# Seven block products for eight in the up-projection of a two-layer decoder trunk: four K blocks of every second strip pair, spread among the plain tiles of two strips

## The chip, the cores and the metric

The kernel runs on one core of one Trainium2 chip. The metric is the device time of one execution in microseconds. The core's engines work side by side, each through a queue of its own: TensorE (PE) multiplies matrices, VectorE (DVE) and ScalarE (ACT) work on elements, GpSimd (POOL) and SyncE (SP) issue transfers here. An instruction that needs another engine's result waits for it at the head of its queue.

## The reference

Two layers over 256 tokens of width 2048. Layer 0 has stick-breaking attention, layer 1 dilated window attention over shared keys and values; each is followed by a gated feed-forward part with a causal convolution and a gate on a per-layer embedding. The change touches the feed-forward part alone, and of it only the product with `w_up`:

```
D_FF = 5632
def causal_depthwise_conv(u, w, bias):        # width 3, along the tokens
    ...
def conv_ffn(h, w_up, conv_w, conv_b, w_down):
    u = causal_depthwise_conv(h @ w_up, conv_w, conv_b)
    gate, val = u[..., :D_FF], u[..., D_FF:]
    return (jax.nn.silu(gate) * val) @ w_down
```

`h` is the normed stream, 256 x 2048; `w_up` is 2048 x 11264. All inputs are 32-bit floats.

## The kernel before, in words

**The work of a matmul.** K, the summed dimension of 2048, is cut into 16 blocks of 128; the tokens into two blocks of 128; the columns of a weight into strips of 512. For 32-bit accuracy every operand is split in a high and a low part, and a block product is three matmuls into one bank of PSUM: low x high, high x low, high x high (`add_block`, lines 339 to 341 before, 342 to 344 after). The tokens' parts are made once; they are the tiles `h`, one for each K block. The weights' parts are made tile by tile.

**A strip.** `weights` (from line 274, line 285 for the transfer) loads a raw buffer of four K blocks of a strip, 1 MB, through SyncE's queue into one of four buffers (`raw`). Two K blocks at a time make a tile: ScalarE copies it into a high part (`whi`, line 302), VectorE subtracts that to get the low part (`wlo`, line 303). There are four buffers for each. So a strip has 8 tiles of 12 matmuls (two K blocks, two token blocks, three matmuls), 96 in all. `strip_v` runs a strip, with its two sums (`accv`, one bank for each token block) in a pool of five banks; one more tile, `two`, holds two banks, and one bank is left for other uses.

**A strip pair.** Strip s gives gate columns, strip s + 11 (`s + FB // 4`) value columns. `products` yields the strips in turn, gate and value alternating. When a strip's sums are complete, ScalarE scales them out of PSUM (`scaled`, line 406), VectorE transposes them in blocks (line 240), and GpSimd sends them to memory and back (lines 243 and 251), which turns the tokens into the free dimension. `finish_strip` convolves a strip one strip later (lines 771 to 780). For a value strip it also multiplies with the gate (line 793) and splits the result into four blocks for the down-projection.

**Parts.** A layer's 11 strip pairs come in two parts, 5 pairs and then 6, each followed by the down-projection of its part. In a layer's first part the first pair starts on the 12 K blocks that are ready (`late` in `products`).

**Order.** The program is written in one stream; a scheduler puts it into the engines' queues by priority. Splits of weights have a high priority (`tc.high_priority`), so that they stand ahead of the convolutions of the strip before. Waits are set by tile: whoever uses a tile waits for the instructions that wrote or read it before.

Of the kernel before, what the change touches and what calls it, by code (L numbers as in the profile page):

```python
# [47 lines left out]
MAGIC = 1.5 * 2.0 ** 23  # L48


def _two_pi_parts():
# [12 lines left out]

RAW = 4
WARM = 9
NRING, NRAW, NWSP = 40, 4, 4
AHEAD = 200
PI_PARTS = _two_pi_parts()

# [2 lines left out]
def tile_trunk(ctx, tc, head_d, xT_d, x_d, pT_d, pos_d, vec_d, cst_d, csb_d, wqkv, wo_a, wkv, wq_b, wo_b, wup, wdn, wpg, wpp, gfin_d, out_d):  # L73
# [11 lines left out]
    def nm(s):  # L85
        uid[0] += 1
        return f"{s}_{uid[0]}"
# [143 lines left out]
    def four(s):  # L231

        return tt(s, (P, 4 * S), tag="four", bufs=3)
# [99 lines left out]
            add_block(ps[o], xs[k], min(o, 1), hi[:, c], lo[:, c], k == 0 and not begun, ends and k == n - 1)  # L333
        return ps

    def add_block(ps, x, t, hi, lo, first, final):
        xh = x[:, t * P : (t + 1) * P]
        xl = x[:, S + t * P : S + (t + 1) * P]
        nc.tensor.matmul(ps, xl, hi, start=first, stop=False)  # L339
        nc.tensor.matmul(ps, xh, lo, start=False, stop=False)  # L340
        nc.tensor.matmul(ps, xh, hi, start=False, stop=final)  # L341

    def two_strips(W, strips, xs, before, block):

# [11 lines left out]
    def products(jobs, xs, late=None, at=0, then={}, side=2):  # L356

        jobs = list(jobs)
        if late is not None:
            n = len(xs)

            def add():
                with tc.issue_after(last["high"]), tc.issue_after(last["low weights"]):
                    late()

            def before(k0):
                if k0 == at:
# [16 lines left out]
            ready = None  # L389
            if at is None:  # L390
                W, s, base = jobs[0]
                ready = list(weights(W, s, 4, base=base + n))
                add()
            for b, (W, s, base) in zip(begun, jobs):
                yield strip_v(W, s, xs[n:], base + n, begun=b, ready=ready)
                ready = None
            jobs = jobs[side:]
        for W, s, base in jobs:
            yield strip_v(W, s, xs, base)

    def scaled(ps, rc, room):

# [357 lines left out]
    def ffn(i, xs, late, rc):  # L760
        cv = V_CONV + i * 4 * 2 * FB

        def taps(r, j, n=1):
            c = cv + r * 2 * FB + j
            return vec[:, c : c + n]

        def conv_turned(j, z, y):

            runs = y.rearrange("p o (a r) -> p o a r", r=32)
            for o in range(4):  # L770
                nc.scalar.activation(runs[:, o], z[:, :, o], AF.Identity, scale=taps(2, j + o), bias=taps(3, j + o))
                for d in (1, 2):
                    c = runs[:, o, :, d:]
                    nc.vector.scalar_tensor_tensor(c, z[:, :, o, : 32 - d], taps(2 - d, j + o), c, op0=OP.mult, op1=OP.add)  # L774
            for d in (1, 2):
                over = tt("over", (P, 7, 4, 2), bufs=2)[:, :, :, :d]
                w = taps(2 - d, j, 4).unsqueeze(1).unsqueeze(3).to_broadcast([P, 7, 4, d])
                nc.vector.tensor_tensor(over, z[:, :7, :, 32 - d :], w, op=OP.mult)
                c = y.rearrange("p o (a r) -> p a o r", r=32)[:, 1:, :, :d]
                nc.vector.tensor_tensor(c, c, over, op=OP.add)  # L780

        def part(strips, late=None):

            gs = []
            gate = [None]

            def finish_strip(value, s, z):
                y = four("val" if value else "gate").rearrange("p (o c) -> p o c", o=4)
                conv_turned(4 * s + value * FB, z, y)
                if not value:  # L790
                    gate[0] = y
                    return nc.scalar.activation(y, y, AF.Silu).ins
                nc.vector.tensor_tensor(y, y, gate[0], op=OP.mult)
# [23 lines left out]
        half = FB // 4 // 2  # L817
        gs, late, _ = part(range(half), late)
# [221 lines left out]
```

## Time and profile before

| | |
|---|---|
| time, median of 3 runs | 2302.58 us (2302.34 to 2302.81) |
| span of the profiled execution, first to last instruction | 2298.6 us; the median lies 4.0 us above it |
| up-projection, layer 0 | 377.5 to 595.1 us and 703.9 to 965.1 us |
| up-projection, layer 1 | 1471.3 to 1689.5 us and 1798.3 to 2059.5 us |
| busy in 703.9 to 965.1 us (261.2 us) | PE 261.2, DVE 179.05, ACT 145.9, POOL 38.27 us |

The profiled execution has no other time than its span. In the profile's rows stand the start, the duration, the engine, the line, the operation and the tiles (out<-in). "Busy" merges overlapping instructions of an engine; a matmul's row includes its latency, so that rows of neighbouring matmuls overlap. In the waits, "A <- B: total, times, longest" means that A stood idle until B was done. In stretch tables there is one column of busy time for each engine, and (xN) counts instructions.

### The profile page before, as it was taken

How to read it: one execution, taken by the hardware profiler on the slowest of the kernel's cores; microseconds unless marked ns; L12 is line 12 of the kernel's file. 1: busy time of each engine (PE TensorE's matmuls, PEld its weight loads, DVE VectorE, ACT ScalarE, POOL GpSimd, SP SyncE). 2: the span in 40 equal slices, each digit the busy share in tenths (PEclk: the TensorE clock that was granted, in tenths of full speed). 3: DMA queues.
4: the chain of work that ended last, by engine and by line, in shares of the span. 5: the costliest groups of instructions: out<-in, count | busy, mean ns of one | idle time of the engine just before them, and what ended most of it. 6: DMA issues, size and time to landing. Idle time of an engine off the chain costs nothing.

```text
span 2298.6 us, 27859 instructions
## 1 busy us (share of the span) xinstructions
PE 2286.6 (99%) x10197; PEld 1893.6 (82%) x10197; DVE 1514.4 (66%) x2205; ACT 1257.3 (55%) x1680; POOL 328.4 (14%) x575
## 2 busy tenths in 40 slices
PE   9999999999999999999999999999999999999998
PEld 7888888888888888888888888888888888888887
DVE  7666666676754767765677665767675476776565
ACT  6554555655534555644565554565553465554554
POOL 0311111111100111101111331211110011110100
PEclk9999999999999999999999999999999999999999
DMA  8777667767656677767577776777765577776763
GB/s 308 254 236 250 221 240 249 247 239 246 223 199 208 241 245 240 244 205 246 205 263 240 252 262 216 262 253 242 237 237 188 215 237 243 244 238 211 239 226 119
DMA packets 98346, 538.44 MB, mean 234 GB/s; under 512 B 16672, under 2 KB 17568, under 8 KB 46752
## 3 DMA queue, kind: packets, MB, share of 16 engines
q1 hardware_dynamic: 63360, 435.46, 54.2%
q0 software_dynamic: 32560, 95.98, 14.0%
q10 hardware_dynamic: 2288, 5.21, 0.6%
q8 instruction: 80, 1.31, 0.2%
q14 instruction: 58, 0.48, 0.1%
HBM read 486.52 MB, written 50.07 MB: 233 GB/s over the span
## 4 chain that ended last, share of the span: by engine, by line
PE 97%; DMA 1%; ACT 1%; DVE 0%; issue 0%; POOL 0%; SPq 0%; ACTq 0%; DVEq 0%; POOLq 0%
PE accv L340 32%; PE accv L341 31%; PE accv L339 31%; PE two L420 1%; PE two L341 0%; PE two L340 0%; PE two L339 0%; DMA turned<-there 0%; DMA there<-y 0%; PE keys L420 0%; ACT whi L302 0%; DVE wlo L303 0%; DMA vec<-in_head 0%; ACT h L140 0%; POOL turned L251 0%
## 5 line engine op out<-in xcount | busy, mean ns | idle before, releaser
L303 DVE TENSOR_TENSOR wlo<-raw,whi 128x1024 fp32r<-128x1024 f32 (+1 forms) x824 | 1001.7, 1216 | 696.0 <-ACT whi L302 694.9
L302 ACT ACTIVATE whi<-raw 128x1024 fp32r<-128x1024 f32 (+1 forms) x824 | 867.8, 1054 | 910.4 <-PE accv L341 886.7
L341 PE MATMUL accv<-whi,h 128*128 128x512 f32 x2328 | 905.3, 389 | 0.0
L339 PE MATMUL accv<-whi,h 128*128 128x512 f32 x2328 | 904.1, 388 | 0.9 <-ACT whi L302 0.6
L340 PE MATMUL accv<-wlo,h 128*128 128x512 f32 x2328 | 904.6, 389 | 0.1
L339 PEld LDWEIGHTS accv<-whi,h 128*128 128x128 f32 x2328 | 437.0, 188 | 92.0 <-ACT whi L302 1.3
L340 PEld LDWEIGHTS accv<-wlo,h 128*128 128x128 f32 x2328 | 437.0, 188 | 91.5 <-DVE wlo L303 1.4
L341 PEld LDWEIGHTS accv<-whi,h 128*128 128x128 f32 x2328 | 437.1, 188 | 89.6
L243 POOL DMA_DIRECT2D there<-y x162 | 91.7, 566 | 1305.5 <-DVE y L240 1288.5
L339 PE MATMUL accv<-whi,g 128*128 128x512 f32 x704 | 273.9, 389 | 0.0
L340 PE MATMUL accv<-wlo,g 128*128 128x512 f32 x704 | 273.9, 389 | 0.0
L341 PE MATMUL accv<-whi,g 128*128 128x512 f32 x704 | 273.9, 389 | 0.0
L251 POOL DMA_DIRECT2D turned<-there x324 | 190.0, 593 | 430.2 <-DMA there<-y 208.0
L339 PEld LDWEIGHTS accv<-whi,g 128*128 128x128 f32 x704 | 132.1, 188 | 27.5
L341 PEld LDWEIGHTS accv<-whi,g 128*128 128x128 f32 x704 | 132.1, 188 | 27.5
L340 PEld LDWEIGHTS accv<-wlo,g 128*128 128x128 f32 x704 | 132.1, 188 | 27.3
L240 DVE STREAM_TRANSPOSE y<-u 128x512 f32<-128x512 f32 x122 | 85.4, 703 | 1.8 <-DMA there<-y 1.4
L339 PE MATMUL accv<-whi,o 128*128 128x512 f32 x200 | 78.0, 390 | 0.0
L341 PE MATMUL accv<-whi,o 128*128 128x512 f32 x200 | 77.9, 390 | 0.0
L340 PE MATMUL accv<-wlo,o 128*128 128x512 f32 x200 | 77.8, 389 | 0.0
L406 ACT ACTIVATE u<-accv,rcol 128x512 f32<-128x512 f32 x102 | 69.2, 678 | 13.7 <-PE accv L341 13.7
L774 DVE SCALAR_TENSOR_TENSOR val<-turned,vec,val 128x248 f32<-128x248 f32 (+1 forms) x176 | 72.2, 462 | 0.0
(163 smaller groups left out, 1179.6 us busy)
## 6 DMA issues: line engine op xcount, KB each, us to landing
raw<-in_wup SPq DMA_DIRECT2D x176, 1024.0 KB, 5.1
raw<-in_wdn SPq DMA_DIRECT2D x88, 1024.0 KB, 4.8
there<-y POOLq DMA_DIRECT2D x171, 256.0 KB, 5.0
turned<-there POOLq DMA_DIRECT2D x324, 128.0 KB, 4.8
raw<-in_wqkv SPq DMA_DIRECT2D x40, 1024.0 KB, 6.6
raw<-in_wpg SPq DMA_DIRECT2D x32, 1024.0 KB, 4.8
raw<-in_wkv SPq DMA_DIRECT2D x24, 1024.0 KB, 5.3
raw<-in_wo_a SPq DMA_DIRECT2D x16, 1024.0 KB, 5.2
```

Of the source, the lines that this page charges most:

```text
L240: last["turned"] = nc.vector.transpose(y.rearrange("p (b o r) -> p o b r", b=4, o=4), strip.rearrange("p (o b c) -> p o b c", o=4, b=4)).ins
L243: nc.gpsimd.dma_start(there[t * P : (t + 1) * P], y)
L251: nc.gpsimd.dma_start(z[32 * b : 32 * b + 32].rearrange("p a o r -> p a (o r)"), back[b])
L302: last["high"] = nc.scalar.activation(hi[:, c], r, AF.Copy).ins
L303: last["low weights"] = nc.vector.tensor_tensor(lo[:, c], r, f32(hi[:, c]), op=OP.subtract).ins
L339: nc.tensor.matmul(ps, xl, hi, start=first, stop=False)
L340: nc.tensor.matmul(ps, xh, lo, start=False, stop=False)
L341: nc.tensor.matmul(ps, xh, hi, start=False, stop=final)
L406: last["out"] = nc.scalar.activation(u, ps[t], AF.Copy, scale=rc[:, t : t + 1]).ins
L420: run.append(nc.tensor.matmul(*args, skip_group_check=True, **kw).ins)
L774: nc.vector.scalar_tensor_tensor(c, z[:, :, o, : 32 - d], taps(2 - d, j + o), c, op0=OP.mult, op1=OP.add)
```

## The change

For every second strip pair the first four of the 16 K blocks are multiplied in another way. The 256 tokens x 512 K values are a 2 x 2 grid of blocks A (two token blocks, two halves of two K blocks). The weights of gate strip s + 1 and value strip v + 1 over these K blocks are a 2 x 2 grid B (two halves of K, two strips). The four blocks of the result C are formed by seven products of sums of blocks instead of eight plain ones:

- `block_sums` makes the four sums of A once for each layer, and splits them (tiles `sum`).
- `Seven.load` fetches the raw buffers of both strips when the value strip v before them begins; they stay in two of the four raw buffers.
- `first` to `fourth` do four products among the plain tiles of strip v, ahead of its tiles 1, 3, 5 and 7 (`HEADS8`). VectorE makes the sums of B in place in the raw buffers (line 439); each factor is split as a tile of weights is, into the same four pairs of buffers (lines 445 and 446). The results lie in `two` (`c11` in its first bank, `c21` in its second) and in two banks named `seven` (`c12`, `c22`). ScalarE copies `c11` and `c12` aside (lines 478 and 485). After the fourth product VectorE combines: line 495 adds `c22` to the first copy, 496 adds that to `c21`, 497 writes `c22` as the second copy minus `c21`, 498 subtracts from `c12`.
- `fifth`, `sixth` and `seventh` add three more products into `c11`, `c21` and `c12`, among the plain tiles of strip s + 1, ahead of its tiles 0, 1 and 3 (`TAILS`).
- Strip s + 1 goes on in `c11` and `c21`, strip v + 1 in `c12` and `c22`, with the 12 K blocks left (6 tiles of 12 matmuls each).

Product by product it is six matmuls (two K blocks, three each). It happens for pairs 3 and 5 of a layer's first part and for pairs 2, 4 and 6 of its second, ten times in all. `HEADS6` is never used. The ring of small buffers grows from 40 to 42, and a tile `part` for the two copies shares the space of `e`. Nothing outside the feed-forward parts moves on any engine, and SyncE and GpSimd issue the same number of transfers.

The core of the diff:

```diff
-    def add_block(ps, x, t, hi, lo, first, final):
+    def add_block(ps, x, t, hi, lo, first, final, again=False):
...
+    class Seven:
...
+        def first(self):
+            gates = two_banks()
+            self.c11, self.c21 = gates[:, 0], gates[:, 1]
+            self.c12, self.c22 = (bank("seven", "acc") for _ in range(2))
+            both = tt("part", (P, 1024), tag="e", bufs=1)
+            self.p, self.q = both[:, :512], both[:, 512:]
+            w = self.parts(self.b11)
+            self.t, self.u = self.b11, self.b12
+            self.add(self.t, self.b11, self.b12)
+            self.add(self.u, self.b12, self.b22)
+            self.product(self.c11, self.token(0, 0), w, True)
+            with tc.high_priority(offset=AHEAD):
+                nc.scalar.activation(self.p, self.c11, AF.Copy)
...
+        def fourth(self):
+            w = self.parts(self.t)
+            self.add(self.t, self.t, self.b21)
+            self.product(self.c22, self.sums[2], w, True)
+            with tc.high_priority(offset=AHEAD):
+                nc.vector.tensor_tensor(self.p, self.c22, self.p, op=OP.add)
+                nc.vector.tensor_tensor(self.c21, self.c21, self.p, op=OP.add)
+                nc.vector.tensor_tensor(self.c22, self.q, self.c21, op=OP.subtract)
+                nc.vector.tensor_tensor(self.c12, self.c12, self.p, op=OP.subtract)
+
+        def fifth(self):
+            self.product(self.c11, self.token(2, 0), self.parts(self.b21))
+
+        def sixth(self):
+            self.product(self.c21, self.token(2, 1), self.parts(self.t))
+
+        def seventh(self):
+            self.product(self.c12, self.sums[3], self.parts(self.b22))
...
-            ups = products([(wup[i], s + v * FB // 4, 0) for s in strips for v in range(2)], xs, late, None)
+            def up_strips():
+                W, now = wup[i], None
+                for j, s in enumerate(strips):
+                    v = s + FB // 4
+                    after = Seven(W, s + 1, v + 1, xs, sums) if j % 2 == (late is not None) and s + 1 in strips else None
...
+                    yield strip_among(W, s, xs, now.go_on() if now else {}, now and [now.c11, now.c21], base)
+                    yield strip_among(W, v, xs, after.begin(tiles) if after else {}, now and [now.c12, now.c22], base)
+                    now = after
+
+            ups = up_strips()
```

**TensorE's queue where a strip ends, before.** The place is layer 0, the end of the second pair's value strip (`accv_3605`) and the start of the next gate strip (`accv_3779`). The rows are the first two matmuls of its last tile and of the next strip's first two tiles; the ten between them have no waits.

```order
L339 MATMUL accv_3605<-whi_3721,h_3297 128x512 [waits Activation_49]
L340 MATMUL accv_3605<-wlo_3722,h_3297 128x512 [waits DVE_49]
...
L339 MATMUL accv_3779<-whi_3775,h_2694 128x512 [waits Activation_49]
L340 MATMUL accv_3779<-wlo_3776,h_2694 128x512 [waits DVE_49]
...
L339 MATMUL accv_3779<-whi_3793,h_2700 128x512 [waits Activation_49]
L340 MATMUL accv_3779<-wlo_3794,h_2700 128x512 [waits DVE_49]
```

Every tile's first matmul waits for ScalarE's high part, its second for VectorE's low part.

**The same place in the change.** `seven_3643` is `c22`, `two_3641` holds `c11` and `c21`. The rows: the last matmul of the fourth product; the start of the value strip's last tile (`accv_3617`); the fifth product; the next strip's first tile; the sixth product; the second tile.

```order
L455 MATMUL seven_3643<-whi_3782,sum_3087 128x512
L342 MATMUL accv_3617<-whi_3797,h_3315 128x512 [waits Activation_49]
L343 MATMUL accv_3617<-wlo_3798,h_3315 128x512 [waits DVE_49]
...
L455 MATMUL two_3641<-whi_3849,h_2700 128x512 [waits DVE_49,Activation_49]
L455 MATMUL two_3641<-wlo_3850,h_2700 128x512
...
L342 MATMUL two_3641<-whi_3861,h_2862 128x512 [waits Activation_49]
L343 MATMUL two_3641<-wlo_3862,h_2862 128x512
...
L455 MATMUL two_3641<-whi_3877,h_2700 128x512 [waits Activation_49]
L455 MATMUL two_3641<-wlo_3878,h_2700 128x512
...
L342 MATMUL two_3641<-whi_3887,h_2868 128x512 [waits Activation_49]
L343 MATMUL two_3641<-wlo_3888,h_2868 128x512 [waits DVE_49]
```

One plain tile stands between the fourth and the fifth product. The fifth product's first matmul waits for both engines, and the low parts `wlo_3850`, `wlo_3862` and `wlo_3878` have no wait of their own; `wlo_3888` is the first that has one again.

**VectorE's queue there, before.** The end of the same value strip and the start of the next gate strip (the names are those of the fence on TensorE before; `y` are the blocks to be turned).

```order
L303 TENSOR_TENSOR wlo_3722<-raw_3703,whi_3721 128x1024 [waits Activation_49]
L303 TENSOR_TENSOR wlo_3776<-raw_3773,whi_3775 128x1024 [waits DMAHW2_49,Activation_49]
L303 TENSOR_TENSOR wlo_3794<-raw_3773,whi_3793 128x1024 [waits Activation_49]
L303 TENSOR_TENSOR wlo_3812<-raw_3809,whi_3811 128x1024 [waits DMAHW3_49,Activation_49]
L240 STREAM_TRANSPOSE y_3742<-u_3737 128x4x4x32 [waits DMASW4_49,Activation_49]
```

Low parts follow each other, each behind its high part.

**VectorE's queue there, in the change.** From the low part of the last plain tile on; `part_3644` holds the two copies, `seven_3642` is `c12`.

```order
L306 TENSOR_TENSOR wlo_3798<-raw_3764,whi_3797 128x1024 [waits Activation_49]
L446 TENSOR_TENSOR wlo_3850<-raw_3619,whi_3849 128x1024 [waits Activation_49]
L306 TENSOR_TENSOR wlo_3862<-raw_3859,whi_3861 128x1024 [waits DMAHW4_49,Activation_49]
L495 TENSOR_TENSOR part_3644<-seven_3643,part_3644 128x512 [waits PE_49]
L446 TENSOR_TENSOR wlo_3878<-raw_3619,whi_3877 128x1024 [waits Activation_49]
L496 TENSOR_TENSOR two_3641<-two_3641,part_3644 128x512 [waits DVE_49]
L498 TENSOR_TENSOR seven_3642<-seven_3642,part_3644 128x512
L497 TENSOR_TENSOR seven_3643<-part_3644,two_3641 128x512 [waits DVE_49]
L306 TENSOR_TENSOR wlo_3888<-raw_3859,whi_3887 128x1024 [waits Activation_49]
```

The four combinations have come in among the low parts, with the sixth product's low part between the first and the second of them; line 498 stands ahead of line 497. The other nine places have the same rows in the same order.

More of the change, by code (lines that the diff above doesn't have):

```diff
@@ L334, in strip_v @@
         return ps
[L336 removed]
+    def add_block(ps, x, t, hi, lo, first, final, again=False):
         xh = x[:, t * P : (t + 1) * P]
         xl = x[:, S + t * P : S + (t + 1) * P]
[L339 to L341 removed]
+        nc.tensor.matmul(ps, xl, hi, start=first, stop=False, skip_group_check=again)
+        nc.tensor.matmul(ps, xh, lo, start=False, stop=False, skip_group_check=again)
+        nc.tensor.matmul(ps, xh, hi, start=False, stop=final, skip_group_check=again)
     def two_strips(W, strips, xs, before, block):
@@ L399, in products, with block_sums @@
             yield strip_v(W, s, xs, base)
+    def block_sums(xs):
+        f = four("whole").rearrange("p (k c) -> p k c", k=4)
+        for k in range(4):
+            nc.vector.tensor_tensor(f[:, k], f32(xs[k][:, :S]), f32(xs[k][:, S:]), op=OP.add)
+        (a11, a21), (a12, a22) = ((f[:, k : k + 2, :P], f[:, k : k + 2, P:]) for k in (0, 2))
+        m = four("sums").rearrange("p (q i c) -> p q i c", q=4, i=2)
+        nc.vector.tensor_tensor(m[:, 0], a21, a22, op=OP.subtract)
+        nc.vector.tensor_tensor(m[:, 1], a11, a21, op=OP.subtract)
+        nc.vector.tensor_tensor(m[:, 2], m[:, 0], a11, op=OP.subtract)
+        nc.vector.tensor_tensor(m[:, 3], m[:, 2], a12, op=OP.add)
+        out = []
+        for q in (0, 2):
+            hi, lo = (rt("sum", dt=F32R) for _ in range(2))
+            src = m[:, q : q + 2].rearrange("p q i c -> p (q i c)")
+            nc.scalar.activation(hi, src, AF.Copy)
+            nc.vector.tensor_tensor(lo, src, f32(hi), op=OP.subtract)
+            for j in range(2):
+                out.append([[t[:, (2 * j + i) * P : (2 * j + i + 1) * P] for t in (hi, lo)] for i in range(2)])
+        return out
@@ new lines, in tile_trunk, with __init__, add, parts @@
+    class Seven:
+        def __init__(self, W, s0, s1, xs, sums):
+            self.strips = W, s0, s1
+            self.sums = sums
+            self.token = lambda k, t: [[xs[k + i][:, c + t * P : c + (t + 1) * P] for c in (0, S)] for i in range(2)]
+        def add(self, out, a, b):
+            with tc.high_priority(offset=AHEAD):
+                nc.vector.tensor_tensor(out, a, b, op=OP.add)
+        def parts(self, r):
+            hi = wsp.tile([P, 2, 512], F32R, tag="hi", name=nm("whi"))
+            lo = wsp.tile([P, 2, 512], F32R, tag="lo", name=nm("wlo"))
+            with tc.high_priority(offset=AHEAD):
+                last["high"] = nc.scalar.activation(hi, r, AF.Copy).ins
+                last["low weights"] = nc.vector.tensor_tensor(lo, r, f32(hi), op=OP.subtract).ins
+            return hi, lo
+        def product(self, ps, left, w, first=False):
+            for i in range(2):
+                xh, xl = left[i]
+                hi, lo = w[0][:, i], w[1][:, i]
+                for j, (x, y) in enumerate(((xl, hi), (xh, lo), (xh, hi))):
+                    begins, ends = first and i == j == 0, first and i == 1 and j == 2
+                    nc.tensor.matmul(ps, x, y, start=begins, stop=ends, skip_group_check=True)
+        def load(self):
+            W, s0, s1 = self.strips
+            raws = []
+            for s in (s0, s1):
+                raw = wraw.tile([P, RAW, 512], F32, tag="raw", name=nm("raw"))
+                nc.sync.dma_start(raw, W[s, 0])
+                raws.append(raw)
+            (self.b11, self.b21), (self.b12, self.b22) = ((r[:, :2], r[:, 2:]) for r in raws)
+        def first(self):
[9 more added lines that the diff above has]
+            self.product(self.c11, self.token(0, 0), w, True)
+            with tc.high_priority(offset=AHEAD):
+                nc.scalar.activation(self.p, self.c11, AF.Copy)
+        def second(self):
+            w = self.parts(self.t)
+            self.add(self.t, self.t, self.b22)
+            self.product(self.c12, self.sums[0], w, True)
+            with tc.high_priority(offset=AHEAD):
+                nc.scalar.activation(self.q, self.c12, AF.Copy)
+        def third(self):
+            self.product(self.c21, self.sums[1], self.parts(self.u), True)
+        def fourth(self):
+            w = self.parts(self.t)
+            self.add(self.t, self.t, self.b21)
+            self.product(self.c22, self.sums[2], w, True)
+            with tc.high_priority(offset=AHEAD):
+                nc.vector.tensor_tensor(self.p, self.c22, self.p, op=OP.add)
[8 more added lines that the diff above has]
+            self.product(self.c12, self.sums[3], self.parts(self.b22))
+        def begin(self, tiles):
+            do = [self.first, self.second, self.third, self.fourth]
+            self.hooks = {0: self.load, **dict(zip({8: HEADS8, 6: HEADS6}[tiles], do))}
+            return self.hooks
+        def go_on(self):
+            return dict(zip(TAILS, (self.fifth, self.sixth, self.seventh)))
@@ new lines, in strip_among, with tiles @@
+    def strip_among(W, s, xs, hooks, begun=None, base=0):
+        n = len(xs) - base
+        ps = begun or [bank("accv", "acc") for _ in range(2)]
+        it = weights(W, s, n, base=base)
+        def tiles():
+            for i in range(n // 2):
+                if i in hooks:
+                    hooks[i]()
+                yield next(it)
+        for k, o, hi, lo in (g for group in steps(tiles(), n, 2) for g in group):
+            add_block(ps[o], xs[base + k], o, hi, lo, k == 0 and not begun, k == n - 1, begun is not None)
+        return ps
@@ L817, in ffn @@
         half = FB // 4 // 2
+        sums = block_sums(xs)
         gs, late, _ = part(range(half), late)
```

8 lines of the change are left out of this document (7 added, 1 removed).

## The prediction

> **What bounds the kernel now.** I read the page first: the busy shares, and the chain that ended last.
>
> ```profile
> span 2298.6 us, 27859 instructions
> PE 2286.6 (99%) x10197; PEld 1893.6 (82%) x10197; DVE 1514.4 (66%) x2205; ACT 1257.3 (55%) x1680; POOL 328.4 (14%) x575
> PE 97%; DMA 1%; ACT 1%; DVE 0%; issue 0%; POOL 0%; SPq 0%; ACTq 0%; DVEq 0%; POOLq 0%
> ```
>
> TensorE is busy for 99% of the span and is 97% of the chain. There is nearly no idle time to win; only fewer matmuls can make this kernel shorter, and any new gap in TensorE's queue adds its full length. Next came the stretches table for two neighbouring up-projection strips (a value strip's finish falls into the first, a gate strip's into the second), and the waits inside the second part of layer 0's up-projection (703.9 to 965.1 us).
>
> ```profile
> core 0: us, PE busy (x) PEld busy (x) DVE busy (x) ACT busy (x) POOL busy (x), PEclk, DMA share, GB/s
> 769.20:791.00 21.80, 21.80 (x98) 18.05 (x97) 16.94 (x28) 12.84 (x18) 3.48 (x6) 1.00 0.73 242
> 791.00:812.80 21.80, 21.80 (x98) 18.06 (x97) 14.52 (x23) 12.55 (x15) 3.48 (x6) 1.00 0.72 241
> ```
>
> ```profile
> ACT whi L302 <- PE accv L341: 107.7, 81, 1.7
> DVE wlo L303 <- ACT whi L302: 81.6, 66, 1.6
> ```
>
> TensorE has no gap in either strip. VectorE (DVE) works 14.5 to 16.9 of 21.8 us, ScalarE (ACT) some 12.7. ScalarE waits for TensorE, not the reverse: the split of a weight tile starts when the tile four places earlier has been used up and its buffer comes free. So the helpers run about three tiles ahead, and that lead is the cover under which the change puts its new work.
>
> **What a matmul is worth.** The timeline of TensorE: the first and the last of 57 matmul rows in a row.
>
> ```profile
> 339.68 0.39 PE L340 MATMUL accv<-wlo,o 128*128 128x512 f32 x1
> 352.37 0.39 PE L339 MATMUL accv<-whi,o 128*128 128x512 f32 x1
> ```
>
> 56 steps take 12.69 us, so one matmul costs 0.2266 us of the path; the 0.39 us in each row is its latency, pipelined away. Four K blocks of a strip pair cost 2 strips x 4 K blocks x 2 token blocks x 3 = 48 matmuls. Seven products of two K blocks cost 7 x 2 x 3 = 42. It happens for two of five pairs in a layer's first part and three of six in its second, in two layers: 10 times. **Removed: 10 x 6 = 60 matmuls x 0.2266 = 13.6 us**, 1.36 us each time. This part is certain.
>
> **What is added, and where it is hidden.** Prices from the groups of that stage:
>
> ```profile
> L303 DVE TENSOR_TENSOR wlo<-raw,whi 128x1024 fp32r<-128x1024 f32 x96 | 117.5, 1224 | 81.6 <-ACT whi L302 81.6
> L793 DVE TENSOR_TENSOR val<-val,gate 128x1024 f32<-128x1024 f32 x5 | 6.1, 1226 | 0.2
> L302 ACT ACTIVATE whi<-raw 128x1024 fp32r<-128x1024 f32 x96 | 101.7, 1059 | 107.7 <-PE accv L341 107.7
> L406 ACT ACTIVATE u<-accv,rcol 128x512 f32<-128x512 f32 x23 | 15.6, 680 | 3.6 <-PE accv L341 3.6
> ```
>
> Each time: seven splits where four stood (3 more: 3.7 us VectorE, 3.2 us ScalarE), four weight sums (4 x 1.23 = 4.9 us VectorE), two copies out of PSUM (2 x 0.68 us ScalarE), four combinations (below). In the value strip that carries the first four products, VectorE then has 16.94 + 4 splits and 4 sums (9.8) = 26.8 us, against 120 matmuls = 27.2 us of TensorE. That is full, but it fits: back to back these instructions step faster than their durations add up, as the next rows show, and ScalarE has 12.84 + 4 x 1.06 + 1.4 = 18.5 of 27.2. The next strip has 72 + 18 matmuls = 20.4 us, the one after it 16.3 us, with 14.52 and 16.94 us of VectorE less two splits each, plus three splits and the combinations in the first: both fit. If this cover were gone, each us by which VectorE is late at every product would cost 10 us.
>
> Both weight blocks stay in two of the four raw buffers, and SyncE's queue issues their loads ahead of the value strip's own.
>
> ```profile
> raw<-in_wup SPq DMA_DIRECT2D x176, 1024.0 KB, 5.1
> ```
>
> A buffer is asked for again once its second tile is split, some 4 us before TensorE starts that tile (30 matmuls after its split buffer came free, 6.8 us, less 2.8 for the split); the buffer's next tile is due 42 matmuls (9.5 us) later; 5.1 us to land and 2.3 us to split leave about 6 us spare. GpSimd's queue and everything outside the up-projection stand as before. The sums of the tokens (ten short VectorE instructions a layer) fall into a stretch where VectorE idles: nothing.
>
> **What is added and not hidden.** The order shows one place. The fifth product accumulates onto the first bank of the pair "two"; its first matmul now waits for VectorE, and neither its own low part, nor the next tile's, nor the sixth product's has a wait of its own behind it, though the latter is split between the combinations. So that one wait reaches to the last combination (line 497), which stands just before the next split that is waited for (wlo_3888). The combinations need the fourth product. Between the two, TensorE has one plain tile, 12 matmuls. The order is the same in all ten places, so I time the chain there, on VectorE's queue: low part of the next strip's first tile (wlo_3862), line 495, low part for the sixth product (wlo_3878), lines 496, 498, 497. First the hand-overs, in the timeline of the stage (TensorE, ScalarE, VectorE):
>
> ```profile
> 782.58 0.39 PE L341 MATMUL accv<-whi,h 128*128 128x512 f32 x1
> 783.01 1.06 ACT L302 ACTIVATE whi<-raw 128x1024 fp32r<-128x1024 f32 x1 [1.09 <-PE accv L341]
> 784.10 1.23 DVE L303 TENSOR_TENSOR wlo<-raw,whi 128x1024 fp32r<-128x1024 f32 x1 [0.93 <-ACT whi L302]
> ```
>
> From the start of a tile's last matmul to the split of the tile that takes its buffer 0.43 us, split 1.06, hand-over 0.03. VectorE's steps back to back, and a pair of 128x512 sums that read PSUM:
>
> ```profile
> 778.29 1.23 DVE L793 TENSOR_TENSOR val<-val,gate 128x1024 f32<-128x1024 f32 x1
> 779.44 1.22 DVE L303 TENSOR_TENSOR wlo<-raw,whi 128x1024 fp32r<-128x1024 f32 x1
> 780.57 1.42 DVE L148 TENSOR_TENSOR g<-val,g 128x256 fp32r<-128x256 f32 x4
> ...
> 1456.57 1.27 DVE L753 TENSOR_TENSOR x<-two,x 128x512 f32<-128x512 f32 x2
> 1457.76 1.21 DVE L303 TENSOR_TENSOR wlo<-raw,whi 128x1024 fp32r<-128x1024 f32 x1
> ```
>
> A low part steps 1.13 us, a 128x512 sum 0.60 (1.19 for two), lasting 0.67. Last, TensorE's restart after a wait for VectorE:
>
> ```profile
> 1482.14 0.49 DVE h L141
> 1482.63 0.04 issue
> 1482.67 0.50 PE accv L339
> ```
>
> ```profile
> 1481.97 0.39 PE L341 MATMUL accv<-whi,h 128*128 128x512 f32 x1
> 1482.67 0.50 PE L339 MATMUL accv<-whi,h 128*128 128x512 f32 x1 [0.32 <-DVE h L141]
> 1483.01 0.39 PE L340 MATMUL accv<-wlo,h 128*128 128x512 f32 x1
> ```
>
> 0.04 us to the start, and the first matmul holds the next back for 0.34 instead of 0.23, 0.11 more. The clock of the chain is the last matmul of the tile before the fourth product, whose buffer wlo_3862's tile takes: 0.43 + 1.06 + 0.03 + 1.13 (wlo_3862) + 0.60 (495) + 1.13 (wlo_3878) + 0.60 (496) + 0.60 (498) + 0.67 (497) + 0.04 = 6.29 us. TensorE would reach the fifth product 6 (fourth) + 12 (tile) + 1 = 19 matmuls after that matmul's start, 4.31 us. So it stands for 1.98 us, and loses 0.11 in restarting: **2.1 us a time, 21 us in ten.** wlo_3878 does not slow the chain: its buffer frees with the fourth product, 6 x 0.2266 + 0.43 + 1.06 + 0.03 = 2.88 us, before VectorE is done with line 495 at 3.25.
>
> Bounds. From below: if wlo_3862 were out of the way, the chain would start at the fourth product and still hold 0.43 + 1.06 + 0.03 + 1.13 + 0.60 + 0.60 + 0.67 + 0.04 = 4.56 us against 13 matmuls, 2.95: 1.6 us and the restart, 1.7 in all. From above: no row shows VectorE writing PSUM; if each of the three that do steps 0.1 us slower than the row that only reads it, 2.4 us. I take 2.1, since the order of the queue fixes wlo_3862's place.
>
> **The sum.** -13.6 + 21.0 = +7.4 us on the profiled 2298.6; the timed median, 2302.58, lies 4.0 above that span, so about 2310. With the bounds: +3.4 to +10.4, 2306 to 2313.
>
> The Trainium skill bears on this wait. "PSUM — Partial Sum Buffer", in its section on bank collisions, says that different engines on the same bank and quadrant raise an error, while on different banks they run clean. By that, the fifth product (first bank) need not wait for sums on the second; no run here shows it either way. It is the first rival.
>
> **The rivals.** (1) The fifth product does not really stand for line 497, because only its bank matters. Then the second bank is first due 12 matmuls (2.72 us) after the fifth product starts; the 1.98 us of lateness are covered, and the saving stays whole: 2302.6 - 13.6 = 2289. For it: the fifth product writes another bank than the sums. Against: the wait stands in TensorE's queue, and only its reach is inferred, from later low parts without a wait. If it reached only to line 496, 1.2 us less: 0.9 a time, 2298.
>
> (2) VectorE is the bound in the loaded value strip: it comes to wlo_3862 late, since 26.8 us of 27.2 leave no slack. By steps: the strip's third low part can start 1.3 us into the strip (0.43 + 1.06 + 0.03, less one matmul); up to wlo_3862 stand 13 steps of 1.13 us and the value finish, 16.94 less 8 low parts of 1.22, 7.2 us: 23.2 us. The tile of wlo_3862 is split at 101 matmuls + 0.43 + 1.06 = 24.4. So the rival decides once VectorE is more than 1.2 us slower than that. Each us beyond costs 10: one us gives 2320. Against: the steps add up to less than the durations, and the strip before it is light.
>
> (3) The stalls take the clock down. The warm-up shows what that costs:
>
> ```profile
> 1.20 3.87 PE L122 MATMUL warm<-zero 128*128 128x512 bf16 x9 [1.20 <-DVE zero L119]
> ```
>
> 0.43 us a matmul for nine of them; if nine after each stall ran so, 9 x 0.20 x 10 = 18 us more, 2328. Against: after the 0.70 us step at 1481.97 the rows keep their pace; but a 2 us gap is longer than any in this trace. "TensorE: Matmul & The Clock Gate", section "HAM oscillation" in the Trainium skill, sets the limit at idle gaps of about 3.4 us; by that these stay below it, and the trace, with its one 0.70 us step, agrees as far as it goes.
>
> **How the numbers follow.** The forecast, the wait as worked out: 0.71. Rival 1 in full 0.10, half of it (2298) 0.04. Rival 2: 0.11. Rival 3: 0.04. The likeliest gives 2310.0. Within the forecast the bounds run from 2306 to 2313; with most of rival 2 and a margin for smaller waits I give 2304.5 to 2318, which leaves out rival 1, rival 3 and what is worst of rival 2, under 0.2 together. A measurement of this kernel tells about 0.2% (4.6 us) from no change: 2298.0 to 2307.2. Faster by more: rival 1, 0.10. Within it: the low end of the forecast (a wait under 1.8 us, 0.11) and the half case, 0.15. Slower: the rest of the forecast (0.60), rivals 2 and 3, 0.75.
>
> **What would show it.** Right: 60 matmul rows fewer; ten gaps of about 2 us on TensorE, at the first matmul of line 455 into "two" behind a plain tile, released by VectorE line 497; nowhere else a gap; the clock at 1.00. Wrong: no gap there (rival 1), gaps at the low parts of plain tiles (rival 2), or 0.43 us matmuls behind a gap (rival 3).

## The result, and the profile after

The changed kernel takes 2320.82 us (median of 4 runs, 2319.23 to 2321.57) beside 2302.69 us for the kernel before (4 runs): ratio 1.0081, interval 1.0067 to 1.0095. It is 18 us slower. The forecast was 2310.0 us, with a range of 2304.5 to 2318.0: the direction is right, the size is not. The profiled execution has a span of 2319.1 us, 20.5 more than before, and its granted clock is 0.993 on average.

From the page of the kernel after: the span, the busy shares, and the chain that ended last by engine.

```profile
span 2319.1 us, 27960 instructions
PE 2285.9 (99%) x10137; PEld 1890.0 (81%) x10137; DVE 1624.0 (70%) x2335; ACT 1300.0 (56%) x1734; POOL 328.7 (14%) x575
PE 96%; DVE 2%; ACT 1%; DMA 1%; issue 0%; POOL 0%
```

60 matmul rows are gone (10197 before), but TensorE's busy time fell by 0.7 us only, where 13.6 were to go, and TensorE now has some 33 us outside it where it had 12. So two things happened: it stood still, and some matmuls took longer. The first shows in the question who waited for what at the tile `two` (us, times).

```profile
its engine sat idle before it (us, times) until:
  DVE seven L497: 19.6, 10
```

Ten waits, 1.96 us each, all for VectorE line 497. The first of them, on TensorE and then on VectorE:

```profile
471.56 0.39 PE L344 MATMUL accv<-whi,h 128*128 128x512 f32 x1
473.91 0.47 PE L455 MATMUL two<-whi,h 128*128 128x512 f32 x1 [1.96 <-DVE seven L497]
474.21 0.40 PE L455 MATMUL two<-wlo,h 128*128 128x512 f32 x1
...
475.76 0.63 PE L343 MATMUL two<-wlo,h 128*128 128x512 f32 x1
476.19 0.63 PE L344 MATMUL two<-whi,h 128*128 128x512 f32 x1
```

```profile
469.00 1.23 DVE L306 TENSOR_TENSOR wlo<-raw,whi 128x1024 fp32r<-128x1024 f32 x1 [0.69 <-ACT whi L305]
470.14 0.68 DVE L495 TENSOR_TENSOR part<-seven,part 128x512 f32<-128x512 f32 x1
470.74 1.22 DVE L446 TENSOR_TENSOR wlo<-raw,whi 128x1024 fp32r<-128x1024 f32 x1
471.88 0.69 DVE L496 TENSOR_TENSOR two<-two,part 128x512 f32<-128x512 f32 x1
472.48 0.69 DVE L498 TENSOR_TENSOR seven<-seven,part 128x512 f32<-128x512 f32 x1
473.07 0.69 DVE L497 TENSOR_TENSOR seven<-part,two 128x512 f32<-128x512 f32 x1
```

This is the forecast chain, row by row. The step from 471.56 to 473.91 is 2.35 us where 0.2266 is normal, the next one 0.30: 2.20 us lost a time, 22.0 in ten (forecast 21).

The second thing stands in the last two rows on TensorE: from 475.76 on, a matmul steps 0.43 us. The stretches table, in stretches of 3.41 us, shows why (PE busy first, PEclk third from the end). First around that stall, then around the fourth one, at 848.93 us:

```profile
471.95:475.37 3.42, 1.46 (x7) 1.25 (x8) 3.42 (x6) 3.38 (x6) 0.00 (x0) 1.00 0.64 225
475.37:478.78 3.41, 3.41 (x10) 2.64 (x9) 3.21 (x7) 1.26 (x2) 1.13 (x2) 0.50 0.99 327
478.78:482.19 3.41, 3.41 (x16) 2.81 (x15) 1.84 (x4) 1.99 (x2) 0.00 (x0) 1.00 0.61 221
```

```profile
847.42:850.83 3.41, 1.90 (x9) 1.24 (x7) 3.41 (x6) 2.49 (x4) 0.00 (x0) 1.00 0.14 17
850.83:854.25 3.42, 2.98 (x13) 2.53 (x14) 3.23 (x6) 3.16 (x6) 1.06 (x2) 1.00 0.89 331
854.25:857.66 3.41, 3.41 (x16) 2.83 (x16) 3.41 (x6) 1.72 (x2) 0.07 (x1) 1.00 0.98 335
```

The clock is granted in windows of 3.413 us whose starts in the trace keep one phase through the whole execution. In the first case the stall lies inside one window (1.96 of 3.42 us idle), and the next window has half the clock; then it is whole again. In the second the same stall is cut by a window's end into 1.51 and 0.44 us, and the clock stays. Six of the ten stalls (at 471.6, 561.1, 759.4, 936.8, 1861.8 and 2039.2 us) lost a window so, 1.6 us each: 9.6 us. The other three executions of the change have no trace, but a granted clock of 0.994 each. Less the 7 to 10 us at half clock with which every trace here ends, that leaves room for five or six such windows in each (an estimate).

The whole, from the steps between TensorE's matmuls (us beyond 0.2266 of all steps over 0.25, by stage):

| | first 30 us | up-projection, layer 0 | start of layer 1's feed-forward part (1440 to 1520) | up-projection, layer 1 (from 1520) | elsewhere | all |
|---|---|---|---|---|---|---|
| before | 3.4 | 0 | 0.6 | 0 | 2.5 | 6.5 |
| after | 5.2 | 17.4 | 1.0 | 14.2 | 2.5 | 40.3 |

33.8 us more, less 13.6 for the 60 matmuls, is 20.2 of the 20.5. In the up-projections 31.6 = 22.0 in stalls + 9.6 in half-clock windows. The 1.8 in the first 30 us is a half-clock window that this execution met at 7.7 us, while loading; the 0.4 at the start of layer 1's feed-forward part is a wait for transferred data that the change does not touch; in the profiles of the experiments below it is between nothing and 5.2 us.

### The profile page after: what moved, and what is told of

Read it like the earlier page. It is cut to its first block, busy times and chain, and to the rows that moved or that the text cites. A ratio compares the mean times of both kernels' runs of the same rounds, so it can differ in the third digit from the quotient of the medians.

```text
span 2319.1 us, 27960 instructions
## 1 busy us (share of the span) xinstructions
PE 2285.9 (99%) x10137; PEld 1890.0 (81%) x10137; DVE 1624.0 (70%) x2335; ACT 1300.0 (56%) x1734; POOL 328.7 (14%) x575
## 3 DMA queue, kind: packets, MB, share of 16 engines
q0 software_dynamic: 32560, 95.98, 13.6%
q8 instruction: 79, 1.29, 0.2%
## 4 chain that ended last, share of the span: by engine, by line
PE 96%; DVE 2%; ACT 1%; DMA 1%; issue 0%; POOL 0%
PE accv L343 25%; PE accv L344 25%; PE accv L342 25%; PE two L342 3%; PE two L343 3%; PE two L344 3%; PE two L455 3%; PE seven L344 2%; PE seven L342 2%; PE seven L343 2%; PE two L554 1%; PE seven L455 1%; ACT whi L305 1%; DVE wlo L306 1%; DVE wlo L446 0%; DMA turned<-there 0%
## 5 line engine op out<-in xcount | busy, mean ns | idle before, releaser
L306 DVE TENSOR_TENSOR wlo<-raw,whi 128x1024 fp32r<-128x1024 f32 (+1 forms) x784 | 952.0, 1216 | 573.9 <-ACT whi L305 571.5
L342 PE MATMUL accv<-whi,h 128*128 128x512 f32 (+1 forms) x1688 | 655.6, 389 | 2.5 <-ACT whi L305 1.7
L344 PE MATMUL accv<-whi,h 128*128 128x512 f32 (+1 forms) x1688 | 657.0, 389 | 0.0
L343 PE MATMUL accv<-wlo,h 128*128 128x512 f32 (+1 forms) x1688 | 656.1, 389 | 0.0
L342 PEld LDWEIGHTS accv<-whi,h 128*128 128x128 f32 x1688 | 317.3, 188 | 68.6 <-ACT whi L305 2.2
L343 PEld LDWEIGHTS accv<-wlo,h 128*128 128x128 f32 x1688 | 317.3, 188 | 65.7 <-DVE wlo L306 0.4
L344 PEld LDWEIGHTS accv<-whi,h 128*128 128x128 f32 x1688 | 317.4, 188 | 64.8
L445 ACT ACTIVATE whi<-raw 128x1024 fp32r<-128x1024 f32 x70 | 74.0, 1058 | 63.2 <-PE accv L344 35.5
L446 DVE TENSOR_TENSOR wlo<-raw,whi 128x1024 fp32r<-128x1024 f32 x70 | 85.5, 1221 | 26.3 <-ACT whi L445 26.3
L342 PE MATMUL two<-whi,h 128*128 128x512 f32 x240 | 96.1, 400 | 0.0
L343 PE MATMUL two<-wlo,h 128*128 128x512 f32 x240 | 95.5, 398 | 0.0
L344 PE MATMUL two<-whi,h 128*128 128x512 f32 x240 | 95.1, 396 | 0.0
L342 PE MATMUL seven<-whi,h 128*128 128x512 f32 x240 | 93.4, 389 | 0.0
```

Of the source, the lines that this page charges most:

```text
L306: last["low weights"] = nc.vector.tensor_tensor(lo[:, c], r, f32(hi[:, c]), op=OP.subtract).ins
L342: nc.tensor.matmul(ps, xl, hi, start=first, stop=False, skip_group_check=again)
L343: nc.tensor.matmul(ps, xh, lo, start=False, stop=False, skip_group_check=again)
L344: nc.tensor.matmul(ps, xh, hi, start=False, stop=final, skip_group_check=again)
L445: last["high"] = nc.scalar.activation(hi, r, AF.Copy).ins
L446: last["low weights"] = nc.vector.tensor_tensor(lo, r, f32(hi), op=OP.subtract).ins
```

## The experiments

Theory: the loss is the wait at the fifth product, with the clock it costs; it comes from `c11` and `c21` being two banks of one tile, and from the one plain tile between the fourth and the fifth product. Rivals: VectorE is short of time in the loaded strip; the sums and the new loop cost something; the product itself, not the tile, carries the wait. Each kernel was timed beside the kernel before on the same chip; ratios are to that.

**A bank of its own for each result.**

```diff
-            gates = two_banks()
-            self.c11, self.c21 = gates[:, 0], gates[:, 1]
+            self.c11, self.c21 = bank("seven", "acc"), bank("seven")
```

> c11 and c21 get a bank tile each instead of the two halves of one tile, so that the fifth product no longer waits for the combinations; the first instruction that must wait for them is the next strip's first matmul into c21, 12 matmuls after the fifth product starts (31 after the chain's clock starts, 7.02 us, against a chain of 6.3 to 6.4). Wait theory (the 2.1 us stall at the fifth product, and the half-clock windows that follow it, are all that the change loses): no gap, no half clock, 2302.7 - 13.6 = 2289. Work theory (the added work on VectorE and ScalarE costs by itself): gaps at low parts of plain tiles remain, above 2300.

Measured: 2289.39 us (5 runs), ratio 0.9938 (0.9924 to 0.9951). The first place on TensorE, then on VectorE (line 495 here is line 496 of the change):

```profile
471.25 0.39 PE L344 MATMUL accv<-whi,h 128*128 128x512 f32 x1
471.48 0.39 PE L455 MATMUL seven<-whi,h 128*128 128x512 f32 x1
471.70 0.39 PE L455 MATMUL seven<-wlo,h 128*128 128x512 f32 x1
```

```profile
471.56 0.69 DVE L495 TENSOR_TENSOR seven<-seven,part 128x512 f32<-128x512 f32 x1
...
472.76 0.69 DVE L496 TENSOR_TENSOR seven<-part,seven 128x512 f32<-128x512 f32 x1
```

TensorE goes on at its normal step while VectorE is still combining in the other banks, with every other instruction as in the change. So the wait is no need of the arithmetic or of the chip; it is the double tile's. Without it 12.8 us come out by the medians (2302.2 to 2289.4), and the 13.6 that were to come lie within the interval. The Trainium skill, "PSUM — Partial Sum Buffer", section "PSUM bank collisions raise a hardware error", tells to guard PSUM by bank; these rows, in which the two engines work in different banks at the same time, agree.

**The four products earlier**, ahead of tiles 1, 2, 4 and 6, so that two plain tiles follow the fourth.

```diff
-HEADS8, HEADS6, TAILS = (1, 3, 5, 7), (1, 2, 4, 5), (0, 1, 3)
+HEADS8, HEADS6, TAILS = (1, 2, 4, 6), (1, 2, 4, 5), (0, 1, 3)
```

> The first four products stand ahead of plain tiles 1, 2, 4, 6 instead of 1, 3, 5, 7; the fifth product waits for the same combination as in the change, but 24 matmuls (5.4 us) stand between the fourth and the fifth product instead of 12. Wait theory: the same wait is there and is covered, no gap, no half clock, 2289. If it were the shared tile as such (a cost of touching it, not lateness): stalls as before, about 2320. Work theory: the products stand closer, VectorE is later than before, gaps at low parts, over 2320.

Measured: 2290.43 us (5 runs), ratio 0.9946 (0.9933 to 0.9958). Of the waits at `two` two are left:

```profile
  DVE seven L497: 1.3, 2
```

The double tile does no harm where 24 matmuls cover the chain. VectorE, which does the same work in the same strips, was not short of time.

**Both together.**

> Two tiles of one bank each instead of the double bank, and the earlier products as well (two plain tiles between the fourth and the fifth). Theory (each of the two alone takes the whole wait away): nothing is added by the second, 2289 us, equal within 0.1% to each alone, and the two small gaps that the earlier products alone had left (0.9 and 1.2 us) are gone. Rival (each takes away a part only): 1 us or more below both, 2288 or less.

Measured: 2289.22 us (5 runs), ratio 0.9946 (0.9932 to 0.9961), and no wait at these tiles. The second remedy adds nothing: they remove the same wait.

**The wait filled** with eight matmuls without use (into a spare bank, put behind the last plain tile in the queue). The wait itself stays.

```diff
...
         def fifth(self):
+            ps = bank("warm")
+            for _ in range(8):
+                with tc.issue_after(last["plain"]):
+                    nc.tensor.matmul(ps, self.x[:, :P], self.x[:, :512], start=True, stop=True)
             self.product(self.c11, self.token(2, 0), self.parts(self.b21))
```

(`last["plain"]` is the last matmul of a plain tile, `self.x` a tile of the tokens; the lines that set them are left out here.)

> The change, with eight matmuls of no use (into the spare bank, waiting for nothing) between the last plain tile and the fifth product: 1.8 of the 1.96 us in which TensorE stood idle are filled, the wait for the combinations stays as long. Clock theory (a window of 3.413 us with more than about 1.7 us of idleness is followed by one at half clock, 1.7 us lost each): no half-clock window, 2302.7 - 13.6 + 10 x 2.2 = 2311. If the clock's drops were not tied to idleness, or the rest had another cause: 2320 as in the change, or more by the fillers.

Measured: 2309.39 us (6 runs), ratio 1.0032 (1.002 to 1.0043). The same place:

```profile
470.39 0.39 PE L344 MATMUL accv<-whi,h 128*128 128x512 f32 x1
470.62 1.97 PE L504 MATMUL warm<-h 128*128 128x512 f32 x8
472.73 0.47 PE L455 MATMUL two<-whi,h 128*128 128x512 f32 x1
473.04 0.40 PE L455 MATMUL two<-wlo,h 128*128 128x512 f32 x1
```

From 470.39 to 472.73 it is 2.34 us as before: the fifth product is no earlier. But TensorE does not idle, no half-clock window follows any of the ten, and the kernel is 11 us faster than the change while it does 80 matmuls more. In the up-projections its trace loses 4.0 us at steps and 18.1 in the extra matmuls, 22.1, where the change loses 31.6: the difference, 9.5 us, is the clock's share by itself, and the time that is left is the forecast without it (2310).

**A part of the wait filled**: two matmuls in place of eight.

> Two extra matmuls without use (into a spare bank) stand between the last plain tile and the fifth product, where eight stood in the run that filled the wait; the wait itself stays as long. It cuts TensorE's idle stretch from 1.96 to some 1.5 us in ten places. Theory (the clock of a window is halved only if some 1.9 us or more of the window before, over half of its 3.41, were idle): no window at half clock behind any of the ten, and the same time as with eight, 2309 to 2310 us. Rival (any stall of this kind can cost clock, more often the longer it is): half windows behind some of the ten, 2312 to 2321 us.

Measured: 2314.86 us (5 runs), ratio 1.0052 (1.0039 to 1.0065). The time missed the theory and lies in the rival's range, but the trace shows that it is not there by the rival's cause:

```profile
471.66 0.39 PE L344 MATMUL accv<-whi,h 128*128 128x512 f32 x1
471.89 0.61 PE L504 MATMUL warm<-h 128*128 128x512 f32 x2
474.01 0.47 PE L455 MATMUL two<-whi,h 128*128 128x512 f32 x1 [1.51 <-DVE seven L497]
```

Ten idle stretches of 1.50 us, six of them inside one window, and no half-clock window behind any. In the up-projections the steps lose 19.0 us here and 20 extra matmuls take 4.5, 23.5 together; with eight it is 22.1. The rest of the time lies elsewhere in this execution (2315.9 us): 3.8 us at the start of layer 1's feed-forward part (none with eight), where a stall of 1.96 us for transferred data fell into one window and halved the next, and 1.3 us more in the first 30 us. The four executions without a trace have a granted clock of 0.998 or 0.999, which leaves room for one half-clock window at the most (an estimate, worked out as above); so the stalls took no series of windows from them either. Where they lost the rest of their time stays open.

**The combinations ahead of the sixth product's low part** on VectorE: one low part less in the chain.

```diff
...
-            self.product(self.c21, self.token(2, 1), self.parts(self.t))
+            self.product(self.c21, self.token(2, 1), self.parts(self.t, self.combined))
```

(`self.combined` is that combination, line 497 of the change; in lines left out here, `parts` issues the low part behind it.)

> The sixth product's low part is put behind the combinations on VectorE, nothing else: the chain to the fifth product gets shorter by about 1.0 us (one step of 1.14 less, one hand-over more), the stall 1.2 instead of 2.2 us with the restart, and the idleness about 1.0 us, under the 1.7 that tripped nothing. Wait and clock theory together: 2302.7 - 13.6 + 12 = 2301, no half-clock window. If every stall trips the clock by some chance whatever its length: 2301 plus some six times 1.7, about 2311.

Measured: 2302.06 us (11 runs), ratio 0.9999 (0.9989 to 1.0009).

```profile
470.94 0.39 PE L344 MATMUL accv<-whi,h 128*128 128x512 f32 x1
472.28 0.47 PE L456 MATMUL two<-whi,h 128*128 128x512 f32 x1 [0.95 <-DVE seven L498]
```

The step is 1.34 us, not 2.35: 1.01 shorter, near the 1.13 of a low part. Ten such stalls cost 11.9 us with their restarts, and none a window: the saving and the loss nearly cancel. (The trace has one half-clock window, at 1487.5 us, behind a wait of 4.41 us for transferred data.) (Line 498 here is 497 of the change.)

**The fifth product one tile later**, behind the next strip's first tile.

```diff
-HEADS8, HEADS6, TAILS = (1, 3, 5, 7), (1, 2, 4, 5), (0, 1, 3)
+HEADS8, HEADS6, TAILS = (1, 3, 5, 7), (1, 2, 4, 5), (1, 2, 3)
```

> The fifth product goes one tile later, behind the first tile of the next strip instead of ahead of it; nothing else is changed. Theory (the wait belongs to whatever touches the double bank first after the combinations, and an idle stretch of half a clock window halves the clock in the next): the next strip's first tile stands in the double bank too, so it now carries the wait, and only 12 matmuls are still left between the fourth product and it. VectorE's queue there has three low parts ahead of the combinations instead of two, and one of them waits until the last plain tile of the value strip has given its buffer back, so the chain grows to some 7.4 us against 2.95 us of matmuls: gaps of 4 to 4.5 us in ten places, at the next strip's first tile and not at the fifth product, each followed by one or two windows at half clock (1.7 us each). 2302.3 - 13.6 + 45 + 17 to 34: 2350 to 2368 us. Rival (the wait belongs to the fifth product, by the order of the products): it is then hidden by 12 more matmuls, 2.7 us: 2289 to 2292 us, no gap.

Measured: 2319.37 us (4 runs), ratio 1.0078 (1.006 to 1.0095). The place was as the theory said, the size was not.

```profile
471.47 0.39 PE L344 MATMUL accv<-whi,h 128*128 128x512 f32 x1
473.82 0.47 PE L342 MATMUL two<-whi,h 128*128 128x512 f32 x1 [1.96 <-DVE seven L497]
474.13 0.40 PE L343 MATMUL two<-wlo,h 128*128 128x512 f32 x1
```

The wait has gone over to a plain tile (line 342), since that now touches `two` first; the rival, by which it is the fifth product's own, is refuted. But the gap is the same 1.96 us. I had put three low parts into VectorE's chain; there are two, as before, only that of the fifth product and that of the plain tile have changed places.

These ten stalls test the rule of the clock again. In nine the wait is 1.96 to 2.01 us: the five that lie inside one window are each followed by half the clock, the four that are cut by a window's end (the fuller part 1.36 to 1.89 us) are not. The tenth is the longest, 3.15 us, behind the matmul at 1950.24, since VectorE came to its combinations 1.2 us later there; its windows:

```profile
1949.08:1952.49 3.41, 1.55 (x7) 0.94 (x5) 3.41 (x5) 2.92 (x5) 0.00 (x0) 1.00 0.38 161
1952.49:1955.90 3.41, 2.12 (x9) 1.80 (x10) 3.41 (x5) 1.77 (x4) 0.22 (x1) 1.00 0.83 300
1955.90:1959.32 3.42, 3.42 (x17) 2.82 (x16) 3.28 (x8) 2.12 (x2) 0.91 (x2) 1.00 0.96 285
```

1.86 us idle in the first window, 1.29 in the second, and the clock stays at 1.00. So the length of a gap alone does not decide; what counts is how much of it lies in one window.

**All but the seven products**: the sums, the new loop, the rings and the tile stay; every pair keeps its eight.

```diff
-                    after = Seven(W, s + 1, v + 1, xs, sums) if j % 2 == (late is not None) and s + 1 in strips else None
+                    after = Seven(W, s + 1, v + 1, xs, sums) if False else None
```

> All that the change adds around the products stays (the sums of the token blocks once a layer, the strips run through the new function, two more ring buffers, the larger tile), but no pair uses seven products: the up-projection has its eight products back. Theory (all of the loss is the wait and the clock at the fifth product): the rest costs nothing, 2302.3 us, within 0.1% of the kernel before. Rival (part of the loss is the sums or the new function at the start of each feed-forward part): 2 us or more above it, 2304.5 or more.

Measured: 2301.78 us (12 runs), ratio 0.9997 (0.9988 to 1.0006). They cost nothing that these runs can tell.

**Seven products in every pair that can have them** (16), with two plain tiles before the fifth product.

```diff
-HEADS8, HEADS6, TAILS = (1, 3, 5, 7), (1, 2, 4, 5), (0, 1, 3)
+HEADS8, HEADS6, TAILS = (1, 2, 4, 6), (1, 2, 3, 4), (0, 1, 3)
...
-                    after = Seven(W, s + 1, v + 1, xs, sums) if j % 2 == (late is not None) and s + 1 in strips else None
+                    after = Seven(W, s + 1, v + 1, xs, sums) if j >= (late is not None) and s + 1 in strips else None
```

> Seven products in every strip pair that can have them, 16 instead of 10, with the four products ahead of tiles 1, 2, 4 and 6 of a strip of eight and 1, 2, 3 and 4 of a strip of six, so that two plain tiles (24 matmuls) stand between the fourth and the fifth product. Theory (the only price is the wait, and two tiles hide it): 16 x 1.36 = 21.8 us are saved, 2280.5 us. Rival (VectorE is full when no lighter strip lies between two loaded ones: 179 us busy in the longest part plus six times some 11 us, 245 of 253 us): gaps at the low parts of plain tiles or of the products, 2290 us or more.

Measured: 2306.93 us (12 runs), ratio 1.0019 (1.0008 to 1.0029). 96 matmuls fewer, and no gain. Two gaps of the stage at 770 us:

```profile
773.15 0.39 PE L342 MATMUL seven<-whi,h 128*128 128x512 f32 x1
774.19 0.50 PE L343 MATMUL seven<-wlo,h 128*128 128x512 f32 x1 [0.65 <-DVE wlo L306]
...
776.59 0.39 PE L344 MATMUL seven<-whi,h 128*128 128x512 f32 x1
778.91 0.50 PE L455 MATMUL two<-whi,h 128*128 128x512 f32 x1 [1.94 <-ACT u L540]
```

The one at 774.19 is a low part that comes late, as the rival has it. Behind this one stands not VectorE's own load, though, but a transfer, as ScalarE's row just before shows:

```profile
771.82 1.06 ACT L305 ACTIVATE whi<-raw 128x1024 fp32r<-128x1024 f32 x1 [5.97 <-DMA raw<-in_wup]
```

At 1643.50 and 1925.67 us, where TensorE waits 0.66 and 0.68 us for a low part, VectorE's load and a transfer meet: the transfer had come late (ScalarE waits for it until 1631.99 and 1914.16), and from the next low part on VectorE works without a pause up to the late one, with sums of weights (line 439) among its work and one just ahead.

The one at 778.91 is a wait neither theory had: the next pair's first product wants the double tile while ScalarE still scales the gate strip's sums out of it (line 540). At `two`, the waits for that line are five, 8.4 us.

**Every pair, and a bank for each result.**

> Seven products in all 16 pairs that can have them, with a bank of its own for each result instead of the double bank. Theory (in the run with every pair, four of the gaps, 1.9 us each, came from the double bank still being read out by ScalarE when the next first product wanted it; the rest from VectorE and the loads): those four gaps go, 8 to 10 us with their clock, the gaps at low parts and loads stay: 2296 to 2299 us, above the 2289 us of ten places. Rival (the double bank was the main price there too): the saving of 21.8 us comes out, 2281 to 2285 us.

Measured: 2304.31 us (12 runs, 2297.15 to 2317.56), ratio 1.0011 (0.9998 to 1.0025). In the profiled execution (2297.15 us, the fastest of the twelve) the waits for line 540 are gone and the late low parts remain; from the waits between 703 and 965 us:

```profile
PE seven L343 <- DVE wlo L306: 6.0, 9, 1.2
ACT whi L305 <- DMA raw<-in_wup: 9.2, 5, 6.4
```

That execution is as the theory said (2296 to 2299), the median is not; the other runs have no trace, and what they lost more is open. That two of four raw buffers held in every pair leave the loads too little lead is only argued from that wait. Ten pairs with a bank for each result, 2289.4 us, remain the best version.

## Why the prediction was wrong, step by step

- **Removed, 13.6 us:** right. 60 rows fewer, and 2289.4 us once the wait is gone (2302.2 beside it, 12.8 less).
- **Hidden work, nothing:** right. No gap at a low part of a plain tile in the change, so rival 2 did not happen; the kernel with all but the products takes 0.9997 of the time before.
- **The wait, 2.1 us a time:** right in place, reach and chain; 2.20 measured. The hand-over from VectorE's end (473.76) to TensorE's start (473.91) is 0.15 us, not 0.04, and the restart 0.08, not 0.11. VectorE steps 0.60 us also where it writes PSUM, so the upper bound wasn't needed.
- **Rival 1** did not happen: the wait stood. Its premise holds on the chip, though: with a bank for each result the product ran beside the sums, and its 2289 is what came out.
- **The step that failed is rival 3,** "The stalls take the clock down". I gave it 0.04 and let it stand as another case beside the forecast, at 2328 or not at all. It is a term of the forecast's own sum: a stall that takes 1.93 us or more of one clock window of 3.413 us costs the next one half its clock. It struck six of ten times, 1.6 us each, 9.6 us, and with it 2310 becomes 2320. How many are struck is a matter of luck, of where the windows lie: with two fewer the time would have come inside the range, and the mechanism would still have been missing from the forecast. What I argued against it was one row with a 0.70 us step, too short to tell, and a limit for gaps of about 3.4 us from the Trainium skill, "TensorE: Matmul & The Clock Gate", section "HAM oscillation". Here the measurement differs: 1.96 us were enough where they lay in one window (3.15 us, cut by a window's end, were not). The same page of the Trainium skill, section "What's actually happening", says that the window is 3413 ns long and runs free of the kernel's start; with that the trace agrees (3.413 us, one phase), and with it I could have seen that a rule on gaps must depend on where they fall.
- **Of the signs** that I named, the ten gaps released by line 497 came, and no other gap in the up-projections; "the clock at 1.00" did not come, and "0.43 us matmuls behind a gap" did.

The filled wait shows the two parts one by one: 2309.4 us with the wait alone, 2320.8 with the idle TensorE.

## What to carry to other kernels

A tile that spans two PSUM banks joins their waits: give results that become ready at different times a bank (and a tile) each, or put enough matmuls between the last writer and the next user to cover the whole chain on the other engine. On a TensorE-bound kernel, price a stall of about 2 us at itself plus the chance of a half-clock window behind it; a stall that can't be removed is cheaper when a few matmuls without use break it, as long as they end before the wait does. A scheme of seven products for eight (Strassen's) pays for the matmuls it saves with buffers and low parts: where it took every pair here, transfers, low parts and read-outs came late and ate the gain.

## What the runs showed of the hardware

- In a kernel that keeps TensorE busy otherwise, the clock fell to half for a window of 3.413 us when TensorE was idle for 1.93 us or more of the window before. All 16 stalls or waits in these traces with 1.93 us or more in one window were followed by it (at 1.93 to 1.96 us 13 of 13, three longer waits for transfers too); none of the 32 waits of 0.9 us or more at the double tile with 1.89 us or less in their fuller window was. (Idle as the rows show it, a matmul's latency counted as busy.) Two cases limit this. In the first 30 us, which these counts leave out, a window of the change with 1.70 us idle (from 4.33 us on) was followed by half the clock too, so the limit between 1.89 and 1.93 us is not shown for other work. And behind the longest wait, 5.15 us with a bank for each result, half the clock lasted two windows, although TensorE was idle for 0.98 us only in the first of them. A window at half clock costs 1.6 us here (0.427 us a matmul).
- The windows do not start with the kernel: in the twelve traces the first one begins 0.1 to 3.2 us after the first instruction. So which stalls are hit differs between executions: six of ten in the change's profile, five of ten with the fifth product later, in different places. By these figures a stall of 1.96 us has 1.93 us or more in one window for 1.51 of the 3.413 us in which it can start, 44% (an estimate): four or five hits in ten, some 7 us.
- At the start of layer 1's feed-forward part TensorE waits for transferred data, from nothing (the filled wait) to 5.2 us (a bank for each result), in code that the experiments do not touch; in the latter profile this and the clock behind it lose 8.2 us, and that execution is the longest of its five, 2295.8 us.
